# Six short waits of TensorE on a ScalarE copy, in the projections and the FFN of a transformer layer

## The chip, the cores and the metric

The kernel runs on one core of a Trainium2 chip. The metric is the device time of one execution in microseconds (us), and lower is better. The time before is the median of three executions: 1712.26, 1712.30 and 1729.35 us, so 1712.3 us.

## What is computed

One layer of a transformer with 256 tokens, 2048 features and 16 heads of 128, all in fp32. The reference, cut to what matters here:

```python
h = modulate(x, sh1, sc1)                      # x: 256 tokens x 2048
proj = h @ w_in                                # q, k, v, GLU input, two gates
attn = latent_window_attention(q, k, v, k_c, v_c, lp['attn_sink'])
y_attn = attn_flat @ lp['w_attn_proj']         # 2048 x 2048
y_conv = conformer_conv(...)                   # 31 taps, norm, silu, @ w_conv_proj
mix = (g_attn * y_attn + g_conv * y_conv) @ lp['w_out']
x_new = layer_norm(ALPHA * x + g1 * mix, ...)
g, u = jnp.split(modulate(x_new, sh2, sc2) @ w_ffn_in, 2, axis=-1)   # 2048 x 11264
ffn = (jax.nn.silu(g) * u) @ w_ffn_out         # 5632 x 2048
return layer_norm(ALPHA * x_new + g2 * ffn, ...)
```

The change touches three of these products: the gate of the attention branch (`ga`, columns of `w_in`), the attention projection (`ap`, `w_attn_proj`) and the first matrix of the FFN (`fg` and `fu`, the two halves of `w_ffn_in`).

## The kernel before

Every large product is cut into chunks of 512 output columns, and a chunk into four units of 512 rows of the weight matrix. A unit is loaded from memory as two tiles `raw` of 128x1024. ScalarE copies each into `hi`, a tile in the reduced type fp32r (line 234), and VectorE subtracts to get the rest, `lo` (line 237). A product of fp32 values is then made of three products: hi by hi (line 263), hi of the weights by lo of the activations (line 265) and lo of the weights by hi of the activations (line 266). `mm_ws` does this for one unit with the weights as the stationary operand: 16 blocks of three matmuls of 128x128 by 128x256, so 48 matmuls. `mm_as` (lines 253, 254, 256) does it with the activations stationary and 512 columns, for q, `w_out` and the second FFN matrix (`fo`).

The list `pairs` holds 32 units: four of `ga`, four of `ap`, and so on four times. The list `ffn` holds 88 units, four of `fg`, four of `fu`, and so on eleven times; the first of them is done another way (line 936).

The order on TensorE, SyncE and for long stretches VectorE is the order of the program. ScalarE's order comes from a scheduler by priority. Each engine takes its instructions strictly in that order. A unit's two splits (`hi`, `lo`) are emitted one unit ahead; `hi` has four half-unit buffers, so the second half of the next unit's `hi` can be written only when the unit before the present one has been multiplied. Products to the side (scores, transposes, a row of ones times a vector) use one of two PSUM tiles, `aux`, in turn.

Of the kernel before, what the change touches and what calls it, by code (L numbers as in the profile page):

```python
# [10 lines left out]
AF = mybir.ActivationFunctionType  # L11
# [82 lines left out]
def layer(ctx, tc, x, c, cx, c_ctx, w_mod, b_mod, w_in, attn_sink, conv_w, conv_b, conv_norm_g, conv_norm_b,  # L94
          w_attn_proj, w_conv_proj, w_out, ln1_g, ln1_b, w_ffn_in, w_ffn_out, ln2_g, ln2_b, consts, out):
    nc = tc.nc
    pe, act, dve, sp = nc.tensor, nc.scalar, nc.vector, nc.sync
# [15 lines left out]
    def small(n, name):  # L113
        return sb.tile([P, n], F32, name=name, tag="small" + name, bufs=2)
# [4 lines left out]
    def aux(name):  # L119
        return pp.tile([P, 512], F32, name=name, tag="aux", bufs=2)  # L120
# [13 lines left out]
    ident = cst[:, 0:128]  # L134
    ones = cst[:, 896:1024]
    sel = cst[:, 1024:1026]
# [59 lines left out]
    def unit(kind, src, work, post=None, shape=(P, 4, 512)):  # L196
        u = Unit()
        u.kind, u.src, u.work, u.post, u.shape = kind, src, work, post, list(shape)
        u.after, u.fill, u.extra, u.keep, u.direct, u.shift = [], None, 0.0, False, False, 0
        units.append(u)  # L200
        return u

# [40 lines left out]
    def mm_as(ps, xh, xl, k0, u, first, last, toks=(0, 1), nk=4, cols=None):  # L243
        for ki in range(nk):
            for i, t in enumerate(toks):
# [9 lines left out]
                for o, wh, wl in outs:  # L255
                    pe.matmul(o, b, wh, start=False, stop=l, skip_group_check=True)  # L256

    def mm_ws(ps, xh, xl, k0, u, first, last):
        for ct, ki in [(ct, ki) for a in (0, 2) for ct in range(4) for ki in (a, a + 1)]:
            cs = slice(P * ct, P * ct + P)  # L260
            o = ps[ct // 2][:, 256 * (ct % 2):256 * (ct % 2) + 256]
            k, l = k0 + ki, last and ki == 3
            pe.matmul(o, u.hi[ki][:, cs], xh[:, k, :], start=first and ki == 0 and ct % 2 == 0, stop=False,  # L263
                      skip_group_check=True)
            pe.matmul(o, u.hi[ki][:, cs], xl[:, k, :], start=False, stop=False, skip_group_check=True)  # L265
            pe.matmul(o, u.lo[ki][:, cs], xh[:, k, :], start=False, stop=l, skip_group_check=True)  # L266

    def chunk(lst, mul, w, c0, x2, post, name, rate=0, late=False):
        st = {}
# [2 lines left out]
        for q in range(4):  # L272
            def work(u, q=q):
# [9 lines left out]
                if late and q == 3:  # L283
# [12 lines left out]
                    ln1_turn(0, 2)  # L296
                    post(st["ps"], 1)
            u = unit("w", wsrc(w, 4 * q, c0), work, (lambda: post(st["ps"])) if q == 3 and not late else None)
            u.keep = late and q < 2
            u.shift = WS_SHIFT if mul is mm_ws else AS_SHIFT  # L300
# [671 lines left out]
    def fg_post(j, ps):  # L972
        if j == 0:
            env["hid"] = [t16([P, KT, SEQ], f"hid{i}") for i in range(3)]
        env[f"sgf{j}"] = []
        for i in range(2):
            s = sg(f"fg{j}{i}")
            act.activation(s, ps[i], AF.Silu)
            env[f"sgf{j}"].append(s)

    def fu_post(j, ps):
        for i in range(2):
            k = 4 * j + 2 * i
            o = env["hid"][k // KT][:, k % KT:k % KT + 2, :].rearrange("p k s -> p (k s)")
            dve.tensor_tensor(o, ps[i], env[f"sgf{j}"][i], OP.mult)
# [175 lines left out]
    glu, qs, pairs, gcu, cpu, wou, ffn, fo = ([] for _ in range(8))  # L1161
# [11 lines left out]
    def ga(j):  # L1173
        chunk(pairs, mm_ws, w_in, OFF_GA + 512 * j, hT, lambda ps: gt_post(f"a{j}", ps), f"ga{j}", ROWS[3])
# [17 lines left out]
    for j in range(11):  # L1192
        chunk(ffn, mm_ws, w_ffn_in, 512 * j, h2T, lambda ps, j=j: fg_post(j, ps), f"fg{j}", ROWS[7] if j else 0)
        chunk(ffn, mm_ws, w_ffn_in, FF + 512 * j, h2T, lambda ps, j=j: fu_post(j, ps), f"fu{j}", ROWS[7] if j else 0)
    for hf in range(2):
        for q in range(NF // 2):
            fo.append(ffn_out_unit(hf, q))
# [129 lines left out]
```

## Time and profile before

| | us |
|---|---|
| median of three executions | 1712.3 |
| profiled execution, its own time | 1720.97 |
| its span, first to last instruction | 1719.2 |
| TensorE busy | 1670.1 (97%) |
| VectorE busy | 1258.7 (73%) |
| ScalarE busy | 771.0 (45%) |

The share of busy time says which engine has little room. The chain of waits says which work ended last at each moment. The timeline gives single instructions with their start, their length and the wait ahead of them. The mean length of one matmul in a stretch tells how closely matmuls follow each other there, since the ends of matmuls in the records are modelled from the pipeline.

### The profile page before, as it was taken

What the parts mean: (1) busy time and instruction counts of PE and PEld (TensorE: products, weight loads), DVE (VectorE), ACT (ScalarE), POOL (GpSimd) and SP (SyncE); (2) the same over time, 40 slices, a digit from 0 to 9 for tenths busy, and PEclk for the clock granted to TensorE, in tenths of its full rate; (3) what the DMA queues carried; (4) which work ended last, traced back from release to release, by engine and by line L of the source; (5) the groups of instructions that cost most, each with busy time, mean ns of one, the idle gap of its engine ahead of it and who ended that gap; (6) DMA issues with size and microseconds to landing.
All of it is one profiled execution on the core that took longest, in us unless ns stands there. A gap on an engine that the chain in (4) does not pass through costs nothing.

```text
span 1719.2 us, 29737 instructions
## 1 busy us (share of the span) xinstructions
PE 1670.1 (97%) x12185; PEld 1517.6 (88%) x12185; DVE 1258.7 (73%) x1698; ACT 771.0 (45%) x949; POOL 7.5 (0%) x8
## 2 busy tenths in 40 slices
PE   5999999999999999999999999999999999999997
PEld 3677999877789999999987799999999999888886
DVE  6356699999998899888899657555555545556766
ACT  3223443466664343456334453444444444444551
POOL 0000000000000000000000000000000000000000
PEclk8999999999999999999999999999999999999998
DMA  9996877643347778887899367777777776555561
GB/s 345 316 326 218 284 265 238 208 122 99 101 122 245 245 260 268 265 278 252 310 340 334 125 212 257 250 244 242 241 244 245 242 231 190 196 197 197 198 225 66
DMA packets 190064, 397.10 MB, mean 231 GB/s; under 512 B 11748, under 2 KB 45540, under 8 KB 188644
## 3 DMA queue, kind: packets, MB, share of 16 engines
q1 hardware_dynamic: 188320, 390.20, 69.3%
q10 hardware_dynamic: 1608, 5.01, 0.8%
q8 instruction: 95, 1.56, 0.4%
q14 instruction: 41, 0.34, 0.1%
HBM read 393.06 MB, written 2.10 MB: 230 GB/s over the span
## 4 chain that ended last, share of the span: by engine, by line
PE 85%; DVE 9%; DMA 3%; ACT 1%; issue 1%; SPq 0%; DVEq 0%; ACTq 0%
PE fu L266 5%; PE fu L265 5%; PE fu L263 5%; PE fg L266 5%; PE fg L265 5%; PE fg L263 5%; PE fo L254 4%; PE fo L256 4%; PE fo L253 4%; DVE lo L237 2%; DVE y L728 2%; PE ga L263 2%; PE ap L263 2%; PE ga L265 2%; PE ap L266 2%; PE ga L266 2%
## 5 line engine op out<-in xcount | busy, mean ns | idle before, releaser
L234 ACT ACTIVATE hi<-raw 128x1024 fp32r<-128x1024 f32 x524 | 555.1, 1061 | 695.8 <-PE fu L265 138.5
L237 DVE TENSOR_TENSOR lo<-raw,hi 128x1024 fp32r<-128x1024 f32 x522 | 634.0, 1223 | 280.5 <-ACT hi L234 275.6
L728 DVE SCALAR_TENSOR_TENSOR y<-ub,cwT,y 128x256 f32<-128x256 f32 x480 | 195.6, 479 | 0.0
L263 PE MATMUL fu<-h2hi,hi 128*128 128x256 f32 x704 | 195.5, 278 | 0.0
L266 PE MATMUL fu<-h2hi,lo 128*128 128x256 f32 x704 | 194.3, 276 | 0.0
L265 PE MATMUL fu<-h2lo,hi 128*128 128x256 f32 x704 | 194.3, 276 | 0.0
L266 PE MATMUL fg<-h2hi,lo 128*128 128x256 f32 x688 | 191.6, 278 | 1.9 <-DVE lo L237 1.9
L263 PE MATMUL fg<-h2hi,hi 128*128 128x256 f32 x688 | 191.9, 279 | 0.0
L265 PE MATMUL fg<-h2lo,hi 128*128 128x256 f32 x688 | 191.5, 278 | 0.0
L263 PEld LDWEIGHTS fu<-h2hi,hi 128*128 128x128 f32 x704 | 132.2, 188 | 0.7 <-issue 0.7
L265 PEld LDWEIGHTS fu<-h2lo,hi 128*128 128x128 f32 x704 | 132.2, 188 | 0.7 <-issue 0.7
L266 PEld LDWEIGHTS fg<-h2hi,lo 128*128 128x128 f32 x688 | 130.7, 190 | 2.1 <-DVE lo L237 2.1
L266 PEld LDWEIGHTS fu<-h2hi,lo 128*128 128x128 f32 x704 | 132.2, 188 | 0.0
L263 PEld LDWEIGHTS fg<-h2hi,hi 128*128 128x128 f32 x688 | 130.7, 190 | 0.2 <-issue 0.2
L265 PEld LDWEIGHTS fg<-h2lo,hi 128*128 128x128 f32 x688 | 130.6, 190 | 0.2 <-issue 0.2
L254 PE MATMUL fo<-lo,hr 128*128 128x512 f32 x320 | 122.6, 383 | 0.0
L253 PE MATMUL fo<-hi,hr 128*128 128x512 f32 x320 | 122.6, 383 | 0.0
L256 PE MATMUL fo<-hi,hr 128*128 128x512 f32 x320 | 97.2, 383 | 0.0
L649 DVE SCALAR_TENSOR_TENSOR g<-raw,csil,g 128x1024 f32<-128x1024 f32 x48 | 61.1, 1283 | 37.0 <-DMA raw<-in_w_mod_dram 36.8
L263 PE MATMUL ga<-hhi,hi 128*128 128x256 f32 x256 | 73.5, 287 | 0.0
L263 PE MATMUL ap<-ahi,hi 128*128 128x256 f32 x256 | 73.1, 285 | 0.0
L266 PE MATMUL cp<-yhi,lo 128*128 128x256 f32 x256 | 71.1, 278 | 1.3 <-DVE lo L237 1.3
(287 smaller groups left out, 3782.3 us busy)
## 6 DMA issues: line engine op xcount, KB each, us to landing
raw<-in_w_in_dram SPq DMA_DIRECT2D x176, 512.0 KB, 4.7
raw<-in_w_ffn_in_dram SPq DMA_DIRECT2D x176, 512.0 KB, 4.5
raw<-in_w_mod_dram SPq DMA_DIRECT2D x128, 512.0 KB, 4.5
raw<-in_w_ffn_out_dram SPq DMA_DIRECT2D x88, 512.0 KB, 4.0
wm<-in_w_mod_dram SPq DMA_DIRECT2D x32, 1024.0 KB, 9.1
raw<-in_w_attn_proj_dram SPq DMA_DIRECT2D x32, 512.0 KB, 5.7
raw<-in_w_conv_proj_dram SPq DMA_DIRECT2D x32, 512.0 KB, 4.9
raw<-in_w_out_dram SPq DMA_DIRECT2D x32, 512.0 KB, 6.1
```

The source lines that it names most:

```text
L234: act.activation(hi, src, AF.Copy)
L237: dve.tensor_sub(lo, src, hi.bitcast(F32))
L253: pe.matmul(o, a, wh, start=f, stop=False, skip_group_check=True)
L254: pe.matmul(o, a, wl, start=False, stop=False, skip_group_check=True)
L256: pe.matmul(o, b, wh, start=False, stop=l, skip_group_check=True)
L263: pe.matmul(o, u.hi[ki][:, cs], xh[:, k, :], start=first and ki == 0 and ct % 2 == 0, stop=False, skip_group_check=True)
L265: pe.matmul(o, u.hi[ki][:, cs], xl[:, k, :], start=False, stop=False, skip_group_check=True)
L266: pe.matmul(o, u.lo[ki][:, cs], xh[:, k, :], start=False, stop=l, skip_group_check=True)
L649: dve.scalar_tensor_tensor(a, u.raw[n].rearrange("p a b -> p (a b)"), csil[:, k, 0:1], a, OP.mult, OP.add)
L728: dve.scalar_tensor_tensor(y[:, k, :], src, w, y[:, k, :], OP.mult, OP.add)
```

## The change

A new function `pause` takes an `aux` tile and a tiny tile in SBUF. It multiplies the identity by two columns of constants into columns 0 and 1 of the PSUM tile, and has ScalarE copy these to SBUF. It returns a second tiny product, identity by that copy, into columns 2 and 3. In a unit that is marked, `mm_ws` does the first product ahead of its 48 matmuls and the second behind the first three. Nothing reads the second product. Six units are marked: 1, 3 and 20 of `pairs`, and 2, 4 and 40 of `ffn` (counted from 0).

```diff
--- before.py
+++ after.py
@@ -196,7 +196,7 @@
     def unit(kind, src, work, post=None, shape=(P, 4, 512)):
         u = Unit()
         u.kind, u.src, u.work, u.post, u.shape = kind, src, work, post, list(shape)
-        u.after, u.fill, u.extra, u.keep, u.direct, u.shift = [], None, 0.0, False, False, 0
+        u.after, u.fill, u.extra, u.keep, u.direct, u.shift, u.pause = [], None, 0.0, False, False, 0, False
         units.append(u)
         return u
 
@@ -255,7 +255,15 @@
                 for o, wh, wl in outs:
                     pe.matmul(o, b, wh, start=False, stop=l, skip_group_check=True)
 
+    def pause():
+
+        ps, t = aux("pause"), small(2, "pause")
+        pe.matmul(ps[:, 0:2], ident, sel, start=True, stop=True)
+        act.activation(t, ps[:, 0:2], AF.Copy)
+        return lambda: pe.matmul(ps[:, 2:4], ident, t, start=True, stop=True)
+
     def mm_ws(ps, xh, xl, k0, u, first, last):
+        wait = pause() if u.pause else None
         for ct, ki in [(ct, ki) for a in (0, 2) for ct in range(4) for ki in (a, a + 1)]:
             cs = slice(P * ct, P * ct + P)
             o = ps[ct // 2][:, 256 * (ct % 2):256 * (ct % 2) + 256]
@@ -264,6 +272,9 @@
                       skip_group_check=True)
             pe.matmul(o, u.hi[ki][:, cs], xl[:, k, :], start=False, stop=False, skip_group_check=True)
             pe.matmul(o, u.lo[ki][:, cs], xh[:, k, :], start=False, stop=l, skip_group_check=True)
+            if wait:
+                wait()
+                wait = None
 
     def chunk(lst, mul, w, c0, x2, post, name, rate=0, late=False):
         st = {}
@@ -1192,6 +1203,8 @@
     for j in range(11):
         chunk(ffn, mm_ws, w_ffn_in, 512 * j, h2T, lambda ps, j=j: fg_post(j, ps), f"fg{j}", ROWS[7] if j else 0)
         chunk(ffn, mm_ws, w_ffn_in, FF + 512 * j, h2T, lambda ps, j=j: fu_post(j, ps), f"fu{j}", ROWS[7] if j else 0)
+    for u in [pairs[i] for i in (1, 3, 20)] + [ffn[i] for i in (2, 4, 40)]:
+        u.pause = True
     for hf in range(2):
         for q in range(NF // 2):
             fo.append(ffn_out_unit(hf, q))
```

On TensorE, at the start of unit 40 of `ffn`, there stood (`fu` and `fg` are PSUM tiles of the chunk that ends and of the one that begins; in brackets the engines or DMA queues whose semaphores an instruction waits for):

```order
L266 MATMUL fu_12365<-h2hi,lo_2_12483 128x256
L263 MATMUL fg_12614<-h2hi,hi_0_12592 128x256 [waits Activation_49]
L265 MATMUL fg_12614<-h2lo,hi_0_12592 128x256
L266 MATMUL fg_12614<-h2hi,lo_0_12593 128x256 [waits DVE_49]
L263 MATMUL fg_12614<-h2hi,hi_0_12592 128x256
```

and there stands now, with line numbers of the changed file:

```order
L274 MATMUL fu_12390<-h2hi,lo_2_12508 128x256
L261 MATMUL pause<-cst 128x2
L271 MATMUL fg_12639<-h2hi,hi_0_12617 128x256 [waits Activation_49]
L273 MATMUL fg_12639<-h2lo,hi_0_12617 128x256
L274 MATMUL fg_12639<-h2hi,lo_0_12618 128x256 [waits DVE_49]
L263 MATMUL pause<-pause,cst 128x2 [waits Activation_49]
L271 MATMUL fg_12639<-h2hi,hi_0_12617 128x256
```

One product stands ahead of three matmuls, and one that waits for ScalarE behind them; all else is as it was. On ScalarE, at the same place, the two halves of the next unit's `hi` and what follows stood so:

```order
L234 ACTIVATE hi_0_12606<-raw_12534 128x1024 [waits DMAHW3_49,DVE_49,PE_49]
L234 ACTIVATE hi_2_12610<-raw_12536 128x1024 [waits DMAHW4_49,DVE_49,PE_49]
L234 ACTIVATE hi_0_12668<-raw_12588 128x1024 [waits DMAHW5_49,DVE_49,PE_49]
```

and now:

```order
L234 ACTIVATE hi_0_12631<-raw_12559 128x1024 [waits DMAHW3_49,DVE_49,PE_49]
L234 ACTIVATE hi_2_12635<-raw_12561 128x1024 [waits DMAHW4_49,DVE_49,PE_49]
L262 ACTIVATE pause<-pause 128x2 [waits PE_49]
L234 ACTIVATE hi_0_12698<-raw_12613 128x1024 [waits DMAHW5_49,DVE_49,PE_49]
```

The copy of the two columns stands behind the second half of the next unit's `hi`. On ScalarE at unit 4 of `ffn`, where the gate `fg` of chunk 0 is passed through its silu in two halves (line 978 before, 989 now), it stands between the second `hi` and the second silu:

```order
L989 ACTIVATE fg_10359<-fg_10034 128x512 [waits PE_49]
L234 ACTIVATE hi_2_10371<-raw_10232 128x1024 [waits DMAHW2_49,DVE_49,PE_49]
L262 ACTIVATE pause<-pause 128x2 [waits PE_49]
L989 ACTIVATE fg_10361<-fg_10035 128x512
L234 ACTIVATE hi_0_10434<-raw_10296 128x1024 [waits DMAHW3_49,DVE_49,PE_49]
```

Before, the second silu followed the second `hi` directly. In the other four units the copy stands in the same way: in unit 1 of `pairs` behind the copy of `pv` to `at` and ahead of the split of `at` (line 129), in unit 3 behind the second half of a `hi`, in unit 20 behind the second sigmoid `gta` and ahead of `g` from `g1b` (line 676), and in unit 2 of `ffn` behind the second half of a `hi` and ahead of `h` (line 949). VectorE, SyncE and GpSimd have the same instructions in the same order as before.

## Rows read from the trace of the kernel before

**Rows 1.** Profile page: the span, and the chain that ended last.

```profile
span 1719.2 us, 29737 instructions
...
PE 85%; DVE 9%; DMA 3%; ACT 1%; issue 1%; SPq 0%; DVEq 0%; ACTq 0%
```

**Rows 2.** Line 263 on TensorE, 640 to 710 us: count, duration min/median/max, first and last start.

```profile
L263 PE MATMUL ap<-ahi,hi x107: 281/281/281, 639.7 to 699.8; 128*128 128x256 f32 x107
L263 PE MATMUL ga<-hhi,hi x64: 281/281/281, 654.9 to 677.2; 128*128 128x256 f32 x64
L263 PE MATMUL gc<-hhi,hi x28: 281/281/281, 700.2 to 709.7; 128*128 128x256 f32 x28
```

**Rows 3.** Line 263 on TensorE, 1210 to 1396 us, the same columns.

```profile
L263 PE MATMUL fg<-h2hi,hi x292: 276/276/276, 1209.8 to 1395.8; 128*128 128x256 f32 x146
L263 PE MATMUL fu<-h2hi,hi x256: 276/276/276, 1228.5 to 1380.5; 128*128 128x256 f32 x128
```

**Rows 4.** TensorE's groups, 505.5 to 510.5 us: count, busy us, mean ns of one.

```profile
L265 PE MATMUL ga<-hlo,hi 128*128 128x256 f32 x15 | 4.2, 281 | 0.0
```

**Rows 5.** TensorE's timeline around three waits: start, length, instruction, idle before it.

```profile
868.55 0.39 PE L266 MATMUL cp<-yhi,lo 128*128 128x256 f32 x1 [1.33 <-DVE lo L237]
...
874.44 0.39 PE L266 MATMUL cp<-yhi,lo 128*128 128x256 f32 x1
...
1039.32 0.38 PE L266 MATMUL fg<-h2hi,lo 128*128 128x256 f32 x1 [1.92 <-DVE lo L237]
```

**Rows 6.** TensorE's groups behind the wait that ends at 868.55, 869.2 to 874 us.

```profile
L263 PE MATMUL cp<-yhi,hi 128*128 128x256 f32 x14 | 3.9, 281 | 0.0
```

**Rows 7.** TensorE's groups behind the wait that ends at 874.44, 875.2 to 879.5 us.

```profile
L263 PE MATMUL cp<-yhi,hi 128*128 128x256 f32 x14 | 3.9, 276 | 0.0
```

**Rows 8.** TensorE's timeline: the fourth matmul of each of the six units.

```profile
514.66 0.28 PE L263 MATMUL ga<-hhi,hi 128*128 128x256 f32 x1
...
527.16 0.28 PE L263 MATMUL ga<-hhi,hi 128*128 128x256 f32 x1
...
631.81 0.28 PE L263 MATMUL ap<-ahi,hi 128*128 128x256 f32 x1
...
996.55 0.28 PE L263 MATMUL fg<-h2hi,hi 128*128 128x256 f32 x1
...
1007.43 0.28 PE L263 MATMUL fu<-h2hi,hi 128*128 128x256 f32 x1
...
1207.09 0.28 PE L263 MATMUL fg<-h2hi,hi 128*128 128x256 f32 x1
```

**Rows 9.** ScalarE's timeline at the six units: start, length, instruction, idle before it.

```profile
515.00 1.05 ACT L129 ACTIVATE ahi<-at 128x1024 fp32r<-128x1024 f32 x1
...
526.88 1.06 ACT L234 ACTIVATE hi<-raw 128x1024 fp32r<-128x1024 f32 x1 [0.48 <-PE ga L265]
...
632.12 0.59 ACT L676 ACTIVATE g<-g1b 128x512 f32<-128x512 f32 x1
...
995.84 1.06 ACT L234 ACTIVATE hi<-raw 128x1024 fp32r<-128x1024 f32 x1 [1.83 <-PE fg L265]
996.81 1.49 ACT L949 ACTIVATE h<-n,AB 128x128 f32<-128x128 f32 x4
...
1008.28 0.59 ACT L978 ACTIVATE fg<-fg 128x512 f32<-128x512 f32 x1
...
1206.84 1.06 ACT L234 ACTIVATE hi<-raw 128x1024 fp32r<-128x1024 f32 x1 [1.66 <-PE fu L265]
```

**Rows 10.** ScalarE's groups by form: its 128x2 instructions.

```profile
L594 ACT ACTIVATE sm<-sm 128x2 f32<-128x2 f32 x16 | 3.1, 196 | 0.0
```

**Rows 11.** TensorE's timeline: two tiny fp32 products (four records) in the head.

```profile
48.71 0.50 PE L432 MATMUL modr<-cst,moda 128*128 128x2 f32 x4
```

**Rows 12.** Stretches: length, TensorE busy (instructions), granted clock, DMA share, GB/s.

```profile
1040.90:1044.10 3.20, 3.20 (x17) 0.50 0.88 287
866.00:872.00 6.00, 4.67 (x40) 1.00 0.87 280
```

## Prediction

> **What bounds the kernel now.** I began with the span and the chain that ended last: 1719.2 us, of which 85% is TensorE [rows 1]. Nothing added to TensorE's row of instructions is hidden, unless TensorE would have waited there anyway.
>
> Then I looked at how closely the matmuls follow each other, because 97% busy doesn't say whether TensorE runs at its best pace. It has two. From 640 to 710 us there are 199 blocks of three matmuls whose first starts lie between 639.7 and 709.7: 70.0 us for 198 steps, 0.3535 us for three, 117.8 ns for one [rows 2]. From 1210 to 1396 us there are 548 blocks between 1209.8 and 1395.8: 186.0 us for 547 steps, 113.3 ns for one [rows 3]. The instruction, shape and number of columns are the same. The reader sees it at once in the duration, 281 ns against 276. So a matmul in the **slow pace** costs 4.5 ns more than in the **quick** one. The whole of `pairs` and the first part of `gc` ran slowly, from the start [rows 4] to 710 us; all of the FFN stretch in rows 3 ran quickly.
>
> What changes the pace? I looked at places where TensorE waits and goes on with the same kind of matmul. A wait that ends at 868.55 is followed by 281 ns [rows 5, 6], one that ends at 874.44 by 276 ns [rows 5, 7]. So a wait can change the pace, and to either side. That is all this trace says on what a pause does to it. The pace then holds for a hundred microseconds and more.
>
> **The profiled execution and the median.** The profiled one took 1720.97 us, 8.7 us more than the median of 1712.3. Its slow stretch has 32 units of 48 matmuls and 28 blocks of `gc`, 1,620 matmuls, which cost 1,620 x 4.5 ns = 7.3 us. That is most of the difference, so I read the median as an execution that is quick nearly everywhere. The third execution, 1729.35, fits an FFN that is slow after the wait at 1039 us: about 30 units up to unit 40 and 48 units from there, 78 x 48 x 4.5 ns = 16.8 us, against 17.05 us. These are readings; no trace of those executions is here.
>
> **What the change adds.** Six times it adds four things: a tiny product, a copy on ScalarE, the wait for it, and a second tiny product. What ends the wait is ScalarE's place in line: the copy stands behind work that ScalarE does anyway. For each unit I take the time at which ScalarE reaches the copy, add 0.20 us for a 128x2 instruction [rows 10], and compare it with the start of the unit's fourth matmul in the trace of before [rows 8], which now stands behind the second product. The first product costs nothing of its own where its time, about a quarter of a microsecond, lies inside this wait.
>
> Where the copy stands ahead of an instruction shown in rows 9, I take that one's start. Where it stands behind a `hi`, I take its start plus 0.97 us, the step from 995.84 to 996.81 [rows 9].
>
> - `pairs` 1: 515.00 + 0.20 - 514.66 = 0.54 us
> - `pairs` 3: 526.88 + 0.97 + 0.20 - 527.16 = 0.89 us
> - `pairs` 20: 632.12 + 0.20 - 631.81 = 0.51 us
> - `ffn` 2: 996.81 + 0.20 - 996.55 = 0.46 us
> - `ffn` 4: 1008.28 + 0.20 - 1007.43 = 1.05 us
> - `ffn` 40: 1206.84 + 0.97 + 0.20 - 1207.09 = 0.92 us
>
> Together 4.37 us. The second product: four records of such products take 0.50 us [rows 11], so two take 0.25 us. The start after a wait costs a further 0.11 us, since the waiting matmuls last 0.39 us and not 0.28 [rows 5]. Six times 0.36 us is 2.16 us. The sum is **6.5 us**.
>
> Bounds. Below: with ScalarE free, the first product (0.25 us) and the copy (0.20 us) outlast three matmuls (0.34 us) by 0.11 us, and with 0.36 us that makes 0.47 us each, 2.8 us. Above: each copy meets one more `hi` that came late, 1.06 us each [rows 9], 12.9 us. I stay with 6.5, since it comes from the very instructions ahead of the copies. The time from one engine's end to the other's start I leave out; it lies within these bounds.
>
> Behind the waiting product on TensorE stand the rest of the unit and everything after it; the splits of later units wait for those matmuls, and so move along. ScalarE gets 0.2 us more at six places, while it is busy 45% of the time. No DMA is added and none is moved past another. Later waits don't absorb the 6.5 us: the wait at 1039 us is for VectorE's `lo` [rows 5], whose loads are paced by buffers that TensorE sets free, so it moves along too.
>
> **A wait and the clock.** The idle stretches of the pauses are shorter than 1.1 us. In the trace an idle stretch of 1.33 us left the granted clock at 1.00 (2.4 GHz), and one of 1.92 us was followed by 3.20 us at 0.50 (1.2 GHz) [rows 5, 12]. A stretch of 3.2 us at half clock loses half of it, 1.6 us. So I price the clock at nothing. The Trainium skill, "TensorE: Matmul & The Clock Gate", section "A second HAM failure mode: psum-queue depth-cycling", says that brief idle moments between groups of matmuls can by themselves make the clock go down and up. By that rule up to six falls would add 6 x 1.6 = 9.6 us; the row with 1.33 us speaks against it here.
>
> **Rivals.**
>
> *The pauses leave TensorE in the slow pace* (on the other side: slower). Place: most of all `ffn` 40, behind which 48 units run without a wait of this length. Price: 48 x 48 x 4.5 ns = 10.4 us, and 7.1 us for `pairs` from unit 1 to 710 us (1,572 matmuls). For it: rows 6. Against it: rows 7. With the FFN's tail alone the time is 1718.8 + 10.4 = 1729.2; with `pairs` too, 1736.3. It decides from a slow tail and one more slow stretch on.
>
> *The pauses end a slow stretch that the median also has.* If the profiler itself costs the 8.7 us, then the median has the slow stretch of rows 2 as well, and the first three pauses may end it: 1712.3 + 6.5 - 7.1 = 1711.7. For it: rows 7, a wait behind which a slow stretch became quick. Against it: the time of the slow stretch explains most of the difference between profile and median.
>
> *The clock falls at the pauses*, as by the rule above: 1718.8 + 9.6 = 1728.4.
>
> *The copies come later than I think*, each behind one more late `hi`: 1712.3 + 12.9 = 1725.2.
>
> That the change does nothing can't be: the copy stands behind the `hi` in ScalarE's order, and TensorE waits on it.
>
> **How the numbers follow.** The forecast is 1712.3 + 6.5 = 1718.8, so 1719 us. Against the profiled execution it reads 1720.97 + 6.5 - 7.1 = 1720.4 if the slow stretch ends at the first pause. I give the forecast 0.55, the slow pace 0.22, the ended slow stretch 0.13, the clock 0.05 and late copies 0.05. About 1% is what a measurement of this kernel can tell from no change: 1695 to 1729.4. Slower by over 1%: 0.14 of the slow pace (the tail alone is right at the edge), and 0.03 of the last two: 0.17. Faster by over 1% would need 17 us, which none of the cases gives; 0.03 for what I don't see. Within 1%: 0.80. The range reaches down to the ended slow stretch, 1711, and up to a slow tail with a little more, 1731; what it leaves out is a slow tail with slow `pairs`, and a time below 1711. The forecast's own range is 1715 to 1724.
>
> **What would show it.** In the profile after: six waits on TensorE for the `pause` copy of 0.4 to 1.1 us each, 3.5 to 5.5 us in all; a `hi`, `at`, `gta` or `fg` on ScalarE just ahead of each copy; the granted clock at 1.00 around each; durations of 276 ns in `pairs` behind unit 3 and in `ffn` behind unit 40. I would be wrong if the durations behind a pause are 281 ns, if a pause is followed by a clock of 0.50, or if the waits sum to more than 7 us.

## The result, and the profile after

The changed kernel takes 1734.7 us, the median of 21 executions; the kernel before takes 1718.4 us in 21 executions on the same chip. The ratio is 1.0088, with a 95% interval of 1.007 to 1.0105. So the change costs about 1%, or 16.35 us by the medians, where 6.5 us was predicted; the time lies above the predicted range of 1711 to 1731 us. (The ratio is that of the means, without the two executions of before that are more than 1.5% above its fastest.)

The executions of the kernel before go from 1707.1 to 1735.4 us. The three that stood ahead of the prediction had a median of 1712.3, 6 us below that of all. The changed kernel has 20 of its 21 executions between 1730.3 and 1738.0. The 21st, 1724.8 us, is the profiled one, so the profile below is of the fastest execution. That has to be kept in mind when it is read.

The page of after, the span, the busy times and the chain that ended last:

```profile
span 1723.0 us, 29790 instructions
...
PE 1671.5 (97%) x12209; PEld 1517.9 (88%) x12209; DVE 1258.8 (73%) x1698; ACT 771.1 (45%) x955; POOL 7.5 (0%) x8
...
PE 85%; DVE 8%; DMA 4%; ACT 2%; issue 1%; SPq 0%; DVEq 0%; ACTq 0%
```

Against [rows 1] almost nothing moved between the engines. TensorE's timeline at the second product of each of the six pauses (start, length, instruction, idle before it; `x2` because an fp32 product leaves two records):

```profile
513.15 0.38 PE L263 MATMUL pause<-pause,cst 128*128 128x2 f32 x2 [0.17 <-ACT pause L262]
...
528.21 0.38 PE L263 MATMUL pause<-pause,cst 128*128 128x2 f32 x2 [1.84 <-ACT pause L262]
...
630.42 0.39 PE L263 MATMUL pause<-pause,cst 128*128 128x2 f32 x2
...
993.56 0.38 PE L263 MATMUL pause<-pause,cst 128*128 128x2 f32 x2
...
1005.84 0.38 PE L263 MATMUL pause<-pause,cst 128*128 128x2 f32 x2 [0.66 <-ACT pause L262]
...
1210.58 0.38 PE L263 MATMUL pause<-pause,cst 128*128 128x2 f32 x2 [0.51 <-ACT pause L262]
```

All six waits are short, except the one in unit 3 of `pairs`. ScalarE's timeline there shows why:

```profile
527.04 1.06 ACT L234 ACTIVATE hi<-raw 128x1024 fp32r<-128x1024 f32 x1 [2.58 <-DMA raw<-in_w_attn_proj_dram]
...
528.01 0.15 ACT L262 ACTIVATE pause<-pause 128x2 f32<-128x2 f32 x1
```

The `hi` ahead of the copy waited 2.58 us for a transfer; in [rows 9] the `hi` at this place had waited 0.48 us. The granted clock around three of the pauses (stretch, length, TensorE busy, clock, DMA share, GB/s):

```profile
525.00:531.00 6.00, 4.16 (x35) 1.00 0.84 270
1003.00:1009.00 6.00, 5.34 (x47) 1.00 0.77 236
1208.00:1213.00 5.00, 4.49 (x39) 1.00 0.67 207
```

Last, the pace behind the pauses. TensorE's line of hi by hi matmuls (271 now, 263 before), as in [rows 2, 3]: count, duration min/median/max, first and last start. From 637 to 707, from 1010 to 1209, and from 1212 to 1396 us:

```profile
L271 PE MATMUL ap<-ahi,hi x112: 276/276/684, 636.3 to 696.3; 128*128 128x256 f32 x112
L271 PE MATMUL ga<-hhi,hi x64: 276/276/276, 653.1 to 674.5; 128*128 128x256 f32 x64
...
L271 PE MATMUL fu<-h2hi,hi x308: 281/281/281, 1010.1 to 1209.0; 128*128 128x256 f32 x154
L271 PE MATMUL fg<-h2hi,hi x256: 281/281/281, 1028.4 to 1186.4; 128*128 128x256 f32 x128
...
L271 PE MATMUL fg<-h2hi,hi x286: 276/276/276, 1212.0 to 1395.9; 128*128 128x256 f32 x143
L271 PE MATMUL fu<-h2hi,hi x256: 276/276/276, 1232.4 to 1384.3; 128*128 128x256 f32 x128
```

This is the result in one view. The projections, slow in [rows 2], are quick now. The FFN is slow from the pause in unit 4 to the pause in unit 40, 200 us, at a place where the profile of before is quick throughout. Behind the pause in unit 40 it is quick, in this execution.

The projections did not turn quick at a pause. Behind the long wait in unit 3 the matmuls still last 281 ns, as they do behind the pause in unit 1. They become quick behind the products `g1p` that follow unit 3, and the kernel before has these too. TensorE's groups from 528.7 to 533.7 us, the `g1p` products, and the groups from 536 to 541 us:

```profile
L273 PE MATMUL ga<-hlo,hi 128*128 128x256 f32 x15 | 4.2, 281 | 0.0
...
533.93 1.06 PE L667 MATMUL g1p<-raw,csil 128*32 128x512 f32 x8
...
L273 PE MATMUL ap<-alo,hi 128*128 128x256 f32 x16 | 4.4, 276 | 0.0
```

So of the six pauses three are followed by the slow pace (units 1 and 3 of `pairs`, unit 4 of `ffn`) and three by the quick one (unit 20 of `pairs`, units 2 and 40 of `ffn`).

The two traces laid side by side, each step between the first matmuls of two places, worked out from start times:

```
step                         before    after    difference
start to pairs 0             505.13   503.07     -2.06
pairs 0 to pairs 4            28.41    31.86     +3.45   two pauses, one of them long
pairs 4 to gc                166.62   161.66     -4.96   one pause; quick instead of slow
gc to ffn 1                  288.36   290.18     +1.82
ffn 1 to ffn 5                24.01    24.69     +0.68   two pauses; no stretch at clock 0.50 near 990 us
ffn 5 to ffn 12               41.90    39.57     -2.33   slow, but no wait and no half clock at 1039 us
ffn 12 to ffn 40             152.32   158.43     +6.11   slow instead of quick
ffn 40 to ffn 41               5.44     6.56     +1.12   a pause
ffn 41 to the end            506.97   506.98     +0.01
together                    1719.16  1723.01     +3.85
```

The wait and the stretch of half clock at 1039 us, in [rows 5, 12], belong to that one execution of before: the longest other wait at this place is 0.85 us (the kernel with the pauses in `pairs` alone), and it left the clock at 1.00.

### The profile page after: what moved, and what is told of

It reads as the page before. It is cut to its first block, busy times and chain, and to the rows that moved or that the text cites. A ratio compares the mean times of both kernels' runs of the same rounds, so it can differ in the third digit from the quotient of the medians.

```text
span 1723.0 us, 29790 instructions
## 1 busy us (share of the span) xinstructions
PE 1671.5 (97%) x12209; PEld 1517.9 (88%) x12209; DVE 1258.8 (73%) x1698; ACT 771.1 (45%) x955; POOL 7.5 (0%) x8
## 4 chain that ended last, share of the span: by engine, by line
PE 85%; DVE 8%; DMA 4%; ACT 2%; issue 1%; SPq 0%; DVEq 0%; ACTq 0%
PE fu L274 5%; PE fu L273 5%; PE fu L271 5%; PE fg L273 5%; PE fg L271 5%; PE fg L274 5%; PE fo L256 4%; PE fo L254 4%; PE fo L253 4%; DVE y L739 2%; DVE lo L237 2%; PE mod L460 2%; PE ap L271 2%; PE a L271 2%; PE a L274 2%; PE gc L274 2%
## 5 line engine op out<-in xcount | busy, mean ns | idle before, releaser
L271 PE MATMUL a<-hhi,hi 128*128 128x256 f32 x256 | 72.2, 282 | 0.0
```

## The experiments

Every diff is against the changed kernel. Counts of units "quick" and "slow" are worked out from the start times in the trace: the median step behind a pause is 113.3 or 117.8 ns, with nothing between. In the longer texts of code, `sel` and `ident` are constants in SBUF.

**One part of the change alone.** Three of the six pauses, and the other three:

```diff
-    for u in [pairs[i] for i in (1, 3, 20)] + [ffn[i] for i in (2, 4, 40)]:
+    for u in [ffn[i] for i in (2, 4, 40)]:
```

> Only the pauses in units 2, 4 and 40 of the FFN; those of the projections are taken out. Theory A (pace): a pause leaves TensorE in the slow pace, 4.5 ns more for each matmul, until the next interruption. Units 4 to 39 are 36 x 48 x 4.5 ns = 7.8 us, units 40 to 87 are 10.4 us, and the waits themselves 3.5 us. So the median is 12 to 20 us above that of before, as much as with all six pauses. Theory B (waits): what costs is the six waits themselves and late copies; then these three cost 3 to 5 us.

```diff
-    for u in [pairs[i] for i in (1, 3, 20)] + [ffn[i] for i in (2, 4, 40)]:
+    for u in [pairs[i] for i in (1, 3, 20)]:
```

> Only the pauses in units 1, 3 and 20 of the projections. Theory A (pace): the projections' slow stretch is worth 7 us at most, executions of before have it or not, and the FFN is as before; the median moves by -3 to +6 us. Theory B (waits): the three waits, one of them 2.1 us long in the profile of the changed kernel, cost 4 to 6 us, about half of what all six cost.

With the FFN's three alone the time is 1732.5 us (before, on the same chip: 1717.2), ratio 1.0062 with 1.0031 to 1.0093. With the three of `pairs` alone it is 1715.1 us, ratio 0.9987 with 0.9957 to 1.0017; one execution of 6005.5 us is left out of that ratio. So nearly all of the loss comes from the three pauses in the FFN. In their profile the FFN is slow from 993 us, behind the pause in unit 2, to past unit 40, until 1408 us.

Then one pause each:

```diff
-    for u in [pairs[i] for i in (1, 3, 20)] + [ffn[i] for i in (2, 4, 40)]:
-        u.pause = True
+    ffn[4].pause = True
```

> One pause alone, in unit 4 of the FFN. In both profiles with it the matmuls behind it last 281 ns. Theory A (pace): nothing interrupts TensorE behind it until the FFN's end, since the wait of before at 1039 us is gone when TensorE is slow; 84 units x 48 x 4.5 ns = 18 us, less about 3.8 us for that wait and the half clock behind it, plus 1.4 us for the pause: 15 us above before, as much as all six. Rival (chance, one in four slow): the median is 1 to 2 us above before, with few executions at +15.

```diff
-    for u in [pairs[i] for i in (1, 3, 20)] + [ffn[i] for i in (2, 4, 40)]:
-        u.pause = True
+    ffn[40].pause = True
```

> One pause alone, in unit 40 of the FFN. If the pace behind a pause is a matter of chance, one in four slow as in the kernel with a pause in each unit, the median is 1 to 2 us above before and a quarter of the executions 12 us above it. If it is fixed by what stands ahead, nearly all executions are at the same place: +1 us (quick) or +12 us (slow, 48 units x 48 x 4.5 ns and the pause).

The pause in unit 4 alone gives 1731.2 us against 1716.4, ratio 1.0068 with 1.0029 to 1.0108. The pause in unit 40 alone gives 1717.1 us, ratio 1.0012 with 0.9979 to 1.0044. A single pause in unit 4 costs 14.7 us by the medians (0.3 to 1.1% by the ratio), nearly everything that the change costs. TensorE's timeline in that kernel, at the pause and at the place where the slow stretch ends:

```profile
1005.00 0.38 PE L263 MATMUL pause<-pause,cst 128*128 128x2 f32 x2 [0.66 <-ACT pause L262]
...
1406.25 0.28 PE L274 MATMUL fg<-h2hi,lo 128*128 128x256 f32 x1
1406.36 1.02 PE L686 MATMUL g2b<-g,cst 128*128 128x512 f32 x2
```

Its line of hi by hi matmuls, from 1250 to 1400 and from 1410 to 1469 us:

```profile
L271 PE MATMUL fg<-h2hi,hi x222: 281/281/281, 1253.7 to 1399.7; 128*128 128x256 f32 x111
...
L271 PE MATMUL fg<-h2hi,hi x72: 276/276/276, 1410.0 to 1458.5; 128*128 128x256 f32 x72
```

Three things are to be seen. TensorE sat idle for 0.66 us. The 281 ns behind it last 400 us. And they end at a product of another shape (`g2b`, fp32, 512 columns, which the kernel has anyway), on which TensorE does not wait. The two other profiles whose FFN is slow behind unit 40 become quick at the same product. The account: the unit with the pause takes 6.88 us where a quick unit takes 5.44, 1.4 us more. The slow pace then costs, each step against that of the kernel with pauses in `pairs` alone, whose FFN is quick, 16.96 - 16.32 = 0.64 us from unit 5 to 8, 158.29 - 152.32 = 5.97 us from unit 12 to 40, 0.2 us in unit 40 and 261.01 - 253.76 = 7.25 us from unit 41 to 87. Together 15.5 us, where 14.7 were measured. (Units 8 to 11 are left out, because the other kernel waits there for `lo`, where before waits at 1039 us; with them and the first product the two traces differ by 15.4 us from unit 1 to the end.) Two of the ten executions lie at 1719.6 and 1720.8 us, the other eight above 1728: this pause too can leave TensorE quick, but rarely does.

The profile of the pause in unit 40 alone taught something else. That execution, 1730.3 us, is slow well ahead of its pause:

```profile
L271 PE MATMUL fu<-h2hi,hi x234: 281/281/281, 1049.8 to 1199.9; 128*128 128x256 f32 x117
L271 PE MATMUL fg<-h2hi,hi x192: 281/281/281, 1071.7 to 1184.4; 128*128 128x256 f32 x192
```

Its slow stretch starts at 1041 us, behind a wait of 0.5 us for VectorE's `lo`:

```profile
1040.72 0.38 PE L274 MATMUL fg<-h2hi,lo 128*128 128x256 f32 x1 [0.51 <-DVE lo L237]
```

The kernel before has this wait as well, and in its profile the FFN is quick behind it [rows 3, 5]. So a kernel's own waits can also be followed by either pace.

**Products and copy, without the wait.** The FFN's three pauses with everything but the wait: the second product reads constants and goes into another PSUM tile, so that it has nothing to wait for.

```diff
-        return lambda: pe.matmul(ps[:, 2:4], ident, t, start=True, stop=True)
+        return lambda: pe.matmul(aux("pause2")[:, 2:4], ident, sel, start=True, stop=True)
...
+    for u in [ffn[i] for i in (2, 4, 40)]:
```

> The pauses of units 2, 4 and 40 of the FFN with both tiny products and ScalarE's copy, but the second product multiplies the constants again, into the other PSUM tile, so that TensorE doesn't wait for the copy. Against the kernel with these three pauses and their waits, some 15 us above before. Theory A (the wait changes the pace) with C (a product without a wait brings the quick pace): 1 to 2 us for the products, less the slow FFN that a quarter of the executions of before have: -4 to +2 us, and no execution near +15. Theory B (products and copies cost the time): still 10 us or more above before.

It took 1717.9 us against 1716.1, ratio 0.999 with 0.9964 to 1.0015, and none of its twelve executions is above 1722.8. The FFN in its profile, 1050 to 1470 us:

```profile
L271 PE MATMUL fu<-h2hi,hi x640: 275/276/684, 1051.1 to 1468.2; 128*128 128x256 f32 x160
```

Quick. Products and copy cost nothing that shows; it is the wait that brings the 15 us.

**Many pauses, with and without the wait.** To see how often a pause is followed by either pace, one in each of the units 4 to 87, and the same with two tiny products that wait for nothing:

```diff
-    for u in [pairs[i] for i in (1, 3, 20)] + [ffn[i] for i in (2, 4, 40)]:
+    for u in ffn[4:]:
```

> A pause in each of the 84 units 4 to 87 of the FFN and none elsewhere, to see the pace behind many pauses in one profile. Each costs about 1.3 us, so the time is about 110 us above before. Theory A (pace): behind most pauses the matmuls last 281 ns, whatever the pace ahead of them. Rival (chance): quick and slow come about as often, and a pause in the quick pace is as likely to end quick. Theory B (waits): all units stay at 276 ns.

```diff
-        ps, t = aux("pause"), small(2, "pause")
+        ps = aux("pause")
...
-        act.activation(t, ps[:, 0:2], AF.Copy)
-        return lambda: pe.matmul(ps[:, 2:4], ident, t, start=True, stop=True)
+        return lambda: pe.matmul(ps[:, 2:4], ident, sel, start=True, stop=True)
...
+    for u in ffn[4:]:
```

> As the kernel with a pause in each of the 84 units, but without ScalarE's copy and so without the wait: the second tiny product multiplies the same constants as the first. It costs 84 times four tiny records, about 0.45 us each, so 40 us more than before. Theory A (pace, through the wait): without a wait the pace is kept, 276 ns from unit 4 to 87 or 281 ns throughout. Rival (products): the tiny products themselves change the pace, and units of both paces alternate, as with the wait.

They took 1824.3 and 1754.0 us, one execution each, beside a median of 1717.2 for the kernel before. So a pause costs about (1824.3 - 1717.2) / 84 = 1.28 us, the slow pace behind some of them included, and two tiny products without a wait (1754.0 - 1717.2) / 84 = 0.44 us. Of the 84 pauses 62 are followed by the quick pace and 22 by the slow one; of the 84 pairs of tiny products all 84 by the quick one. How long TensorE's matmuls waited for the copies (us, times), about 0.5 us each, and the granted clock from 1100 to 1300 us in the kernel with 84 pauses, and the hi by hi matmuls, 1005 to 1450 us, in the one without waits:

```profile
  PE pause L263: 41.4, 83
...
1100.00:1300.00 200.00, 184.65 (x1544) 1.00 0.64 193
```

```profile
L270 PE MATMUL fu<-h2hi,hi x618: 276/276/365, 1004.9 to 1449.9; 128*128 128x256 f32 x155
L270 PE MATMUL fg<-h2hi,hi x576: 276/276/365, 1027.2 to 1430.6; 128*128 128x256 f32 x192
```

The granted clock stays at 1.00 (2.4 GHz) through all these waits, from 1010 to 1560 us, so the slow pace is not the clock. All 84 pairs of tiny products had the quick pace ahead of them; that run shows that they leave it quick, not yet that they end a slow one. The Trainium skill, "TensorE: Matmul & The Clock Gate", section "A second HAM failure mode: psum-queue depth-cycling", tells of a kernel in which frequent brief idle moments between groups of matmuls make the clock swing; here 84 of them did not.

**Pause and tiny products in turn.** If the wait makes TensorE slow and the tiny products without a wait make it quick again, the two in turn should show both in every pair. Once with tiny products (first diff), once with one fp32 product of 256 columns in their place (second diff, that function alone):

```diff
+    def go_on():
+        ps = aux("goon")
+        pe.matmul(ps[:, 0:2], ident, sel, start=True, stop=True)
+        return lambda: pe.matmul(ps[:, 2:4], ident, sel, start=True, stop=True)
...
-        wait = pause() if u.pause else None
+        wait = None if not u.pause else pause() if u.pause == 'wait' else go_on()
...
+    for i, u in enumerate(ffn[4:]):
+        u.pause = ('wait', 'go')[i % 2]
```

> In units 4 to 87 of the FFN in turn a pause with its wait and two tiny products without copy and wait. A third of the 42 pauses should leave TensorE slow, some 14. Theory C (a product without a wait brings the quick pace): behind all 42 units with tiny products the matmuls last 276 ns, also where the pause ahead left 281. Theory D (it keeps the pace): the slow ones stay at 281 ns. The time is 42 x 1.3 + 42 x 0.45 = 73 us above before, both ways within 3 us.

```diff
+    def go_on():
+        ps = aux("goon")
+        pe.matmul(ps[:, 0:256], ident, cst[:, 128:384], start=True, stop=True)
```

> As the kernel with pauses and tiny products in turn, but instead of the tiny ones a single fp32 product of 128x256 without a wait, like the column mean behind which the slow stretch of before ended at 712 us. Theory C: behind all 42 of them 276 ns. Theory D: those that began slow stay at 281 ns, as behind the 128x512 products of a row in before. About 42 x 1.3 + 42 x 0.5 = 76 us above before.

They took 1790.8 us both. With tiny products, 40 of the 42 pauses are followed by the slow pace and all 42 pairs of tiny products by the quick one, 40 times out of the slow one. TensorE in this kernel, a pause and the pair of tiny products behind it, each with the groups of the stretch that follows (for these: count, busy us, mean ns):

```profile
1040.90 0.38 PE L268 MATMUL pause<-pause,cst 128*128 128x2 f32 x2 [0.51 <-ACT pause L267]
...
L278 PE MATMUL fg<-h2lo,hi 128*128 128x256 f32 x14 | 3.9, 281 | 0.0
...
1047.11 0.28 PE L261 MATMUL goon<-cst 128*128 128x2 f32 x2
...
L278 PE MATMUL fg<-h2lo,hi 128*128 128x256 f32 x13 | 3.6, 276 | 0.0
```

With the product of 256 columns, only 13 of the 42 pauses are followed by the slow pace, and 41 of 42 of these products by the quick one. So in this stretch a product without a wait ends the slow pace, tiny or wide: 40 times of 40 with the tiny ones, 13 of 13 with the wide one. But the same pause was followed by the slow pace in 40 of 42 cases in one kernel, in 13 of 42 in the other and in 22 of 84 in the one before. The wait alone doesn't decide; something about when it ends does.

The start times say more. Chance it is not: in the kernel with 84 pauses, 20 of the 22 pauses behind which the slow pace follows stand in the first units of chunks, 21 units in all, and unit 4 and unit 40 are among these. The place alone is not it either. Take the three kernels with a copy of two columns, and measure from the start of the last matmul ahead of a pause to the start of its second product. For most pauses this is 1369 or 1370 ns. Of those with the quick pace ahead, all 57 at 1369 ns are followed by the quick pace and 69 of the 78 at 1370 ns by the slow one. In 25 units both kernels in turn have such a pause: with tiny products it is 1370 ns and slow, 25 times of 25; with the wide one 1369 ns and quick, 25 of 25. The records are whole nanoseconds, so about a nanosecond in the end of the wait goes with the outcome.

**The moment at which the wait ends.** The kernel with pauses and tiny products in turn, with a copy that is 2, 4, ... 84 columns wide, so that the wait gets longer by a nanosecond or two from one pause to the next. The first product is changed as well: it is 128 columns wide and not 2, so that there is something to copy.

```diff
+        ps, t, w = aux("pause"), small(128, "pause"), env["w"]
+        env["w"] = w + 2
+        pe.matmul(ps[:, 0:128], ident, ones, start=True, stop=True)
+        act.activation(t[:, 0:w], ps[:, 0:w], AF.Copy)
+        return lambda: pe.matmul(ps[:, 128:130], ident, t[:, 0:2], start=True, stop=True)
```

> As the kernel with pauses and tiny products in turn, where 40 of 42 pauses left TensorE slow, but ScalarE's copy is 2, 4, 6 ... 84 columns wide, so that each wait ends a little later than the one ahead; the pace ahead of each is brought to quick by the tiny products. If the pace is fixed by the moment at which the wait ends, to within some ns, quick and slow should come in turns along the widths. If something else fixes it (the unit, the tile, the pace ahead), all are slow as with the width of 2. If it is chance, no order is seen. About 75 us above before.

It took 1792.5 us. The copies (count, duration min/median/max, first and last start) grow from 156 ns in unit 6 to 222 ns in unit 86, 1.65 ns a pause:

```profile
L268 ACT ACTIVATE pause<-pause x42: 156/188/227, 1006.0 to 1531.2; 128x2 f32<-128x2 f32 x1, 128x4 f32<-128x4 f32 x1, 128x6 f32<-128x6 f32 x1, 128x8 f32<-128x8 f32 x1
```

The pace behind the 42 pauses, in the order of the widths (S slow, F quick):

```
S S S F F F S F F S F F F S S F F S F F F S S F F S S F S S S F S S S F S S S F F S
```

22 of 42 are slow, in short runs, where the kernel with one width had 40 of 42 in the same units. So the longer copies, with the wider first product, turned half of them. That the width orders the outcomes is not shown. Four pauses lengthen the copy by 6.6 ns, and four pauses are also eight units, a pair of chunks. Sorted by place alone, the pauses in units 10, 18, ... 82 are slow 0 times of 10 and those in units 6, 14, ... 86 10 times of 11; the two groups between, 8 of 10 and 4 of 11. In the kernel with the wide product, where the width is fixed, the slow pace recurs every eight units too: 8, 16, ... 80, 10 of 10, and 3 of the other 32. I looked for a period by which the start of the waiting product sorts the two; the best among periods from 2 to 30 ns is 6.67 ns, of which the quick step of 113.3 ns is 17. It was searched for afterwards in one run, and a pattern that repeats every four pauses would give nearly the same figure. The period stays open; widths in another order would settle it.

**Tiny products as a cure.** Since tiny products without a wait leave TensorE quick, a few of them should take from the kernel its slow stretches. First in unit 1 of `pairs` and units 10 and 20 of `ffn`:

```diff
+    for u in (pairs[1], ffn[10], ffn[20]):
```

(and the pair of products without copy and wait, as above)

> No pause; instead the two tiny products without copy and wait in unit 1 of the projections and units 10 and 20 of the FFN, behind the places where before falls into the slow pace (the transposes at 504 us and the wait at 1039 us). Theory C: the slow stretches end there. Cost 1.4 us; gain up to 7 us where the projections were slow, 17 us where the FFN was: the median 3 to 7 us below before, and no execution more than 10 us above the lowest. Theory D (tiny products keep the pace): +1.4 us, with the same spread as before.

It took 1714.6 us against 1716.1, ratio 0.9987 with 0.9962 to 1.0012, less than was expected, and the slowest execution lies 16.9 us above the fastest and not within 10. In the profile the FFN was quick, but the projections were not. TensorE's groups behind the tiny products in unit 1 of `pairs`, 513.6 to 518 us:

```profile
L272 PE MATMUL ga<-hlo,hi 128*128 128x256 f32 x13 | 3.7, 281 | 0.0
```

Here a pair of products without a wait left TensorE slow. They stand right behind the products of the probabilities by the values (`pv`). At this place the kernel with the FFN's three pauses turns from quick to slow with nothing added. The same pair in all units of `pairs`, to see where it works:

```diff
+    for u in pairs[1:] + [ffn[10], ffn[20]]:
+        u.pause = 'go'
```

> Two tiny products without a wait in each of the units 1 to 31 of the projections, and in units 10 and 20 of the FFN; no pauses. In the FFN such products were followed by the quick pace 124 times of 124, but in the kernel with three of them the one in unit 1 of the projections was followed by the slow pace. If that was its place behind the values' product, the later units turn quick and stay so: 276 ns from unit 2 or 3 on. If such products don't help in the projections at all, units stay at 281 ns. 31 x 0.45 us more, 14 us, less up to 7 us.

It took 1727.6 us, in one execution, beside one of 1727.1 of the kernel before. Of the 33 pairs six stand right behind the products for the modulation's rows (`g1p`), and all six are followed by the slow pace, five times out of the quick one. Of the other 27, 26 are followed by the quick pace; the one that is not is again the one behind the values' product. In the profile of before the `g1p` products, with no pair behind them, left the slow pace as it was; in that of after one of them ended it, at 533.93 us. A `g1p`, and the groups behind the pair next to it and behind the pair of the unit after:

```profile
533.92 1.06 PE L672 MATMUL g1p<-raw,csil 128*32 128x512 f32 x8
534.92 0.38 PE L260 MATMUL goon<-cst 128*128 128x2 f32 x2
...
L278 PE MATMUL ap<-alo,hi 128*128 128x256 f32 x15 | 4.2, 281 | 0.0
...
L278 PE MATMUL ap<-alo,hi 128*128 128x256 f32 x15 | 4.1, 276 | 0.0
```

So the cure works in a plain stretch of matmuls and not directly behind those products. Next, the pauses of units 1 and 3 of `pairs` with tiny products in the FFN (the function `go_on` as above):

```diff
+    for u, p in ((pairs[1], 'wait'), (pairs[3], 'wait'), (ffn[10], 'go'), (ffn[20], 'go')):
+        u.pause = p
```

> The pauses of units 1 and 3 of the projections, behind which the projections ran quickly in both profiles that have them, and tiny products without a wait in units 10 and 20 of the FFN, with which no execution was slow there. The waits cost 2.5 us, the products 0.9 us; the slow stretch of the projections is worth 7 us, the slow FFN 17 us in a quarter of the executions. If each part does what it did alone: a median 3 to 6 us below before. If what a pause does hangs on its moment, the projections' gain may be gone: 0 to +3 us.

It took 1715.4 us against 1718.9, ratio 0.996 with 0.9928 to 0.9993, as expected. And tiny products alone, at three places inside plain stretches:

```diff
+    for u in (pairs[3], ffn[10], ffn[20]):
+        u.pause = 'go'
```

> No pause; two tiny products without a wait in unit 3 of the projections and units 10 and 20 of the FFN, all in plain stretches, with no other product just ahead. In the projections such a place brought the quick pace every time, while those behind the modulation row's products or the values' product did not. Cost 3 x 0.45 = 1.4 us; gain 6.4 us where the projections are slow from unit 3 on, and 17 us in the quarter of executions with a slow FFN. The median is 4 to 7 us below before and no execution is above 1724 us.

It took 1711.1 us against 1715.8, ratio 0.9957 with 0.9926 to 0.9987, as expected: 0.4% below the kernel before, clear of 1, and so below the changed kernel too, which was not measured beside it. Its twelve executions lie between 1708.5 and 1714.9, those of the kernel before, on the same chip, between 1707.9 and 1732.0. It doesn't beat the best execution of before; it takes away the bad ones. Its span, and its hi by hi matmuls from 1100 to 1380 us (276 to 277 ns here, at steps of 113.3 ns):

```profile
span 1709.3 us, 29760 instructions
...
L276 PE MATMUL fu<-h2hi,hi x413: 275/277/277, 1099.9 to 1370.5; 128*128 128x256 f32 x138
L276 PE MATMUL fg<-h2hi,hi x411: 275/276/277, 1109.7 to 1379.7; 128*128 128x256 f32 x137
```

One that failed: beside the three pairs of the first of these kernels, tiny products also among the 512-column matmuls of `fo`, whose steps of 217 to 227 ns looked as if they had a better pace in them.

```diff
+                if hf == 0 and q % 2 and q > 1:
+                    pe.matmul(aux('go')[:, 0:2], ident, sel, start=True, stop=True)
```

> The kernel with three such places, and a tiny product without a wait ahead of every second unit of the first half of the second FFN matrix, where the 512-column matmuls start 222.7 ns apart and elsewhere in the kernel 220.0. If the quick pace of 220 ns can be brought there too, 480 matmuls gain 1.3 us in that half and the ten products cost 2.2 us; if not, the pace stays at 222.7 ns and the half is 2.2 us longer.

The step through `fo` went from 228.44 to 231.88 us, 0.34 us for each of the ten products. Nothing came back. In the second half, where no tiny product stands, the steps are even a little longer, 223.6 ns against 222.8. `fo` gains nothing from this.

## Why the prediction was wrong, and where it was right

**The six pauses: right, but for one.** What each pause costs by itself, pace apart, can be taken from the steps of the kernels that have it and those that don't. Unit 40 of `ffn`: its first product stands in the step ahead, 158.43 us where the kernel with unit 4's pause alone has 158.29, and the rest makes its own step 6.56 us in place of 5.44; together 1.26 us. In the same way: unit 1 of `pairs` 0.89 us, unit 3 2.56, unit 20 0.85; units 2 and 4 of `ffn` 0.79 and 1.37. With 0.36 us on each predicted wait the prediction had 0.90, 1.25, 0.87, 0.82, 1.41 and 1.28. Five agree within 0.06 us. In unit 3 the `hi` ahead of the copy came late by its transfer, which the prediction had as a rival for all six and which happened at one. The sum is 7.7 us and not 6.5. TensorE's idle time ahead of the second products is 0.17, 1.84, 0.14, 0.07, 0.66 and 0.51 us, in the order of the units. Unit 3 apart, that is 0.4 us less than each predicted wait. About half of that is the first product and the slower start behind it (0.22 us in unit 40), which lie inside the wait as the prediction had it; the other half comes of counting idle time from the modelled end of the last matmul and not from where the next would start.

**The clock: right.** 1.00 around the pauses. A wait of 1.84 us left it at 1.00, where 1.92 us in the profile of before was followed by 0.50 [rows 5, 12].

**The step that failed is the one on the pace.** The prediction saw the two paces, priced them (4.5 ns a matmul), and saw in [rows 6, 7] that a wait can be followed by either. It then put the pace behind the pauses at nothing in its sum of 6.5 us and kept the slow one as a rival at 0.22. The trace gave little ground for that: of the waits in [rows 5], the one at 868.55 us came out slow, the one at 874.44 quick, and the one at 1039.32, with its stretch of half clock, quick. Each of six pauses fixed the pace anew, two of them ahead of long plain stretches. And the prediction looked for the danger at unit 40, "behind which 48 units run without a wait of this length". The place was unit 4, from which a slow pace runs through unit 40 as well: 1.4 us in the sum, 14.7 us in the measurement with that pause alone.

One of the prediction's signs came true by luck. It named 276 ns in `pairs` behind unit 3. The projections are quick from unit 4 on, but `g1p` made them so; the pauses in units 1 and 3 left 281 ns.

The slow tail behind unit 40 was also sized a little high, 10.4 us. It ends at the `g2b` product at 1406 us, 34 units later, not with the FFN: 7.25 + 0.2 = 7.5 us.

**From the profile to the median.** The profiled execution has a slow FFN up to unit 40 and a quick one behind it. The median is 9.9 us longer. A slow tail behind unit 40 as well, 7.5 us, explains most of that; the rest may be slow projections, up to 5.8 us (the 4.96 of the table, and the 0.85 us of the pause in unit 20). No trace of such an execution of the changed kernel was taken; the kernel with the FFN's three pauses alone was profiled in one, at 1731.7 us, slow on both sides of unit 40.

**The base.** The prediction read the median of three, 1712.3, as "an execution that is quick nearly everywhere". Of 21 executions the median is 1718.4: the kernel before has slow stretches in many of them. No execution of it at 1712 us was profiled; the kernel with three tiny pairs at 1711.1 us is quick nearly everywhere. From the median of 21 the same sum gives 1718.4 + 7.7 = 1726 us with nothing slow that wasn't slow before. The third execution, 1729.35, was read as an FFN that is slow behind the wait at 1039 us. That fits: the profile at 1730.3 us (the pause in unit 40 alone) shows a slow FFN that starts at 1041 us behind that wait.

**Shown and argued.** Shown: the loss comes from the waits in the FFN, and one of them, in unit 4, brings nearly all of it; it is a change of TensorE from steps of 113.3 ns to steps of 117.8 at a granted clock of 1.00; with products and copy but without the wait the FFN stays quick; a product without a wait in a plain stretch of the FFN ends the slow pace; for the same pause in the same unit, 1369 ns were followed by the quick pace and 1370 by the slow one. Not shown: that the width of the copy by itself turns the outcome. Argued only: why unit 4 comes out slow nearly each time. Its copy stands behind a `hi` that itself waits for a matmul, so the wait may end at nearly the same moment of TensorE's own steps in each execution. Open: what in TensorE keeps a pace for hundreds of microseconds, whether there is a period, and why some products bring the slow pace with no wait.

## What to carry to other kernels

In a dense stream of matmuls, look at the step from start to start and not at the busy share: the profiles before and after both read 97% busy, and 4% of a 400 us stretch is more than any wait in it. A short wait on another engine in front of such a stretch has a price that the wait's length doesn't show, so set it where a product of another kind, without a wait, follows soon, or put a pair of tiny products (0.44 us) into the plain stretch behind it, and see in a profile whether the pace is quick there. And where the executions of a kernel spread by 1%, ask for their paces before a median of three is taken as the base.

## What the runs showed of the hardware

- The same matmul, 128x128 by 128x256 in fp32r, has two lasting paces at a granted clock of 1.00: steps of 113.3 and 117.8 ns. A pace holds for up to 400 us, until something other than these matmuls comes between.
- Which one follows a wait goes with about a nanosecond in its end: in three kernels with the same pause and the quick pace ahead, 57 of 57 were quick at 1369 ns from the last matmul to the waiting product, and 69 of 78 slow at 1370.
- Products that wait for nothing end a slow stretch inside the FFN: tiny pairs did it 40 times of 40 in turns with one pause and 22 of 22 in turns with copies of growing width, a wide product 13 of 13. Right behind `g1p` (four products into 32 rows each) a tiny pair was followed by the slow pace, six of six.
- The two paces are most of the spread of the kernel before. On one chip it went from 1707.9 to 1732.0 us, and with three tiny pairs from 1708.5 to 1714.9.
